# Weight quarters summed by accumulating transfers, with the next product's operands traced behind the preceding product

## The chip, the cores and the metric

One core of a Trainium2 chip runs the whole program in one launch. The metric is the device time of the execution in microseconds; lower is better.

## The reference, cut to what matters

512 tokens of width 1024 pass two networks of two layers each, in fp32. The parts around the change are the two kinds of feed-forward layers:

```python
D_FF = -(-(8 * D_MODEL) // (3 * 256)) * 256      # 2816
D_FF_2 = 4 * D_MODEL

def swiglu_ffn(x, w_gate, w_up, w_down):          # first network, both layers
    return (jax.nn.silu(x @ w_gate) * (x @ w_up)) @ w_down

def sq_relu_mlp(h, w_up, w_down):                 # second network, both layers
    u = jax.nn.relu(h @ w_up)
    return (u * u) @ w_down
```

Around them stand mixers, cross attention, sliding-window attention, norms and the residual adds, which the change does not touch.

## The kernel before, in words

Every fp32 product runs as three matmuls of a rounded high half and the remainder (`mm3`: hi x hi at L180, hi x lo at L181, lo x hi at L182; which side is loaded as weights differs). So every operand is split: the high half is a copy on ScalarE (L152, `Copy` to fp32r), the low half a subtraction on VectorE (L153), both in `split`. Weights with a norm's gain are split by `chunk` at L172 (ScalarE) and L173 (VectorE), two 128x512 instructions each.

Weights are loaded in blocks of 512 KB, 256 rows by 512 columns, by SP (L161 in `chunk`, L202 in `raw2`) into `raw`, a pool of 5 buffers, and split into `w`, a pool of 4 (`wsplit`). A buffer is free when the split, or the product, that read it is done. PSUM has 5 banks `mm` and 3 banks `aux` (`xbank`). POOL has its own queue for transfers.

`down_steps` multiplies 1024 hidden columns by 1024 rows of the down weights with 7 products instead of 8: both matrices are cut in quarters (`a11` to `a22`, `block(i, j)`), and products are made of sums of quarters (`s1`, `s2`, `chain`) and added to the residual by `out` (`resid`, L429 and L431). Each product is 24 matmuls. In the order of the program they are called 1, 2, 5, 6, 7, 3 and 4 here. The operands of products 5, 6, 7 and 4 need sums of weight quarters: VectorE takes them at L294 (W01 - W00 into `chain`), L305 (W11 - `chain`), L315 (W11 - W01) and L331 (W10 - `chain`), each 128x1024 and twice a product, for the two halves of a quarter. 18 weight blocks are loaded a call.

It is a generator. `weave` runs one piece of it, up to the next `yield`, then `per` steps of the side generator `hidden`, which computes the next 1024 columns of the hidden layer: `lin_steps` with 24 matmuls a step and, after the last of four steps, the evacuation of the four banks: `silu` at L922 in `ffn`, `relu` at L1048 and a squaring at L1053 in `mlp`. `ffn` calls it twice a layer with two side steps a piece (L941), `mlp` three times a layer with one (L1065): 4 and 6 calls in all.

The order on each engine comes from a scheduler that walks the program in the order in which it is traced. A block under `high_priority(offset=120)` counts as traced 120 instructions earlier. Within an engine everything runs in that fixed order, so an instruction that waits holds all behind it on its engine.

Of the kernel before, what the change touches and what calls it, by code (L numbers as in the profile page):

```python
# [14 lines left out]
ALU = mybir.AluOpType  # L15
AX = mybir.AxisListType

ALPHA = 4.0 ** 0.25
# [54 lines left out]
class Net:  # L73
# [158 lines left out]
        for _ in side:  # L232
            pass

    def down_steps(self, h, W, k0, first, ahead=120):

        nc = self.nc
        early = lambda: self.tc.high_priority(offset=ahead)
        lo, hi = slice(0, 256), slice(256, 512)
        a11, a21, a12, a22 = h[0][:, :, lo], h[0][:, :, hi], h[1][:, :, lo], h[1][:, :, hi]
        sums = self.slot([128, 2, 4, 256], name="sum")
        s1, s2 = sums[:, 0], sums[:, 1]
        chain = self.slot([128, 4, 512], name="chain")
        tt = nc.vector.tensor_tensor

        def left(src):  # L250
            d = self.slot([128, 2, 4, 256], F32R, "A")
            self.split(d[:, 0], d[:, 1], src)
            return d

        def block(i, j):
            return [self.raw2(W, k0 + 4 * i + k, 512 * j) for k in (0, 2)]

        def halves(t):
            return [t[:, 0:2], t[:, 2:4]]

        def product(d, us, banks, start):
            for t in range(2):
                tk = slice(t * 128, t * 128 + 128)
                for k in range(4):
                    u = us[k // 2]
                    self.mm3(banks[t], d[:, 0, k, tk], d[:, 1, k, tk], u[:, 0, k % 2], u[:, 1, k % 2],
                             start and k == 0, k == 3, skip_group_check=not start)

        def out(i, j, banks):
            for t in range(2):  # L270
                self.resid(2 * i + t, banks[t], 512 * j, first and (i, j) not in done)
            done.add((i, j))

        done = set()
        with early():
            d = left(a11)
            us = [self.wsplit(b) for b in block(0, 0)]
        x = [self.xbank([128, 512]) for _ in range(2)]
        product(d, us, x, True)
        out(0, 0, x)  # L280
        yield
        with early():
            d = left(a12)
            us = [self.wsplit(b) for b in block(1, 0)]
        y = [self.xbank([128, 512]), self.bank([128, 512])]
        product(d, us, y, True)
        out(0, 0, y)
        yield
        with early():
            tt(s1, a21, a22, ALU.add)  # L290
            d = left(s1)
            us = []
            for c, p, q in zip(halves(chain), block(0, 1), block(0, 0)):
                tt(c, p, q, ALU.subtract)  # L294
                us.append(self.wsplit(c))
        z = [self.xbank([128, 512]), self.bank([128, 512])]
        product(d, us, z, True)
        out(1, 1, z)
        yield
        with early():  # L300
            tt(s2, s1, a11, ALU.subtract)
            d = left(s2)
            us = []
            for c, p in zip(halves(chain), block(1, 1)):
                tt(c, p, c, ALU.subtract)  # L305
                us.append(self.wsplit(c))
        product(d, us, x, False)
        out(0, 1, x)
        yield
        with early():  # L310
            tt(a21, a11, a21, ALU.subtract)
            d = left(a21)
            us = []
            for p, q in zip(block(1, 1), block(0, 1)):
                tt(p, p, q, ALU.subtract)  # L315
                us.append(self.wsplit(p))
        product(d, us, x, False)
        out(1, 1, x)
        yield
        with early():  # L320
            tt(a12, a12, s2, ALU.subtract)
            d = left(a12)
            us = [self.wsplit(b) for b in block(1, 1)]
        product(d, us, z, False)
        out(0, 1, z)
        yield
        with early():
            d = left(a22)
            us = []
            for c, p in zip(halves(chain), block(1, 0)):  # L330
                tt(c, p, c, ALU.subtract)  # L331
                us.append(self.wsplit(c))
        product(d, us, x, False)
        out(1, 0, x)
        yield

# [86 lines left out]
        nc.vector.scalar_tensor_tensor(dst, x, mv[:, 0:1], g, ALU.subtract, ALU.mult)  # L423
        nc.vector.scalar_tensor_tensor(dst, dst, rs[:, 0:1], b, ALU.mult, ALU.add)

    def resid(self, t, ps, c0, first=False):
        r = self.r[t][:, c0:c0 + 512]
        if first:
            self.nc.vector.scalar_tensor_tensor(r, r, ALPHA, ps, ALU.mult, ALU.add)  # L429
        else:  # L430
            self.nc.vector.tensor_tensor(r, r, ps, ALU.add)  # L431

# [840 lines left out]
```

## Time and profile before

| | |
|---|---|
| median of 3 runs | 2495.14 us (2490.13 to 2496.63) |
| the profiled execution | 2487.76 us, span 2486.0 us |
| mean granted TensorE clock in it | 0.986 |
| busy: TensorE, VectorE, ScalarE, POOL | 97%, 61%, 41%, 7% |
| moved by DMA | 291.92 MB, mean 117 GB/s |
| the chain that ended last | 89% TensorE, 6% VectorE, 3% ScalarE |

The span is the stretch from the first to the last instruction; the execution's own time has 1.8 us around it. The granted clock is a share of TensorE's full 2.4 GHz; 0.50 is 1.2 GHz. L12 is line 12 of the kernel.

### The profile page before, as it was taken

To read this page: it belongs to the slowest core of one execution; us is meant where nothing else is said; L and a number is where in the kernel's file an instruction comes from. 1 tells how busy PE (TensorE), PEld (TensorE's weight loads), DVE (VectorE), ACT (ScalarE), POOL (GpSimd) and SP (SyncE) were. 2 spreads that over 40 slices of the span, in tenths; PEclk is the share of its full clock that TensorE was granted. 3 is DMA by queue.
4 is the path that set the end of the run, shared out by engine and by line. 5 is a ranking of instruction groups with operands and counts; after the bars stand their busy time and mean duration, and the time that the engine had idled before them with its cause. 6 is when DMAs were issued, how large, how long until landed. Compare 5 with 4: busy or idle time off the path is not lost.

```text
span 2486.0 us, 30362 instructions
## 1 busy us (share of the span) xinstructions
PE 2416.0 (97%) x12094; PEld 2012.8 (81%) x12094; DVE 1514.2 (61%) x1994; ACT 1026.8 (41%) x1620; POOL 180.0 (7%) x219
## 2 busy tenths in 40 slices
PE   8989999999999999999999999999999999999998
PEld 8877787887878997887878786888888877888887
DVE  4898666346466766446467432457876467477784
ACT  3653343223333343223334733444444456444443
POOL 1251300000000000000001002200000100000000
PEclk9999999999999999999999999999999989999999
DMA  6323122234334332235334123325543421254451
GB/s 233 110 97 107 54 94 77 88 113 165 110 129 154 127 130 76 94 102 170 110 125 149 61 85 34 102 86 185 186 161 128 152 68 36 69 170 154 151 186 68
DMA packets 148990, 291.92 MB, mean 117 GB/s; under 512 B 9449, under 2 KB 15909, under 8 KB 148592
## 3 DMA queue, kind: packets, MB, share of 16 engines
q1 hardware_dynamic: 146176, 282.17, 34.2%
q0 software_dynamic: 2096, 6.76, 1.4%
q8 instruction: 95, 1.56, 0.3%
q10 hardware_dynamic: 576, 1.05, 0.1%
q14 instruction: 47, 0.39, 0.0%
HBM read 286.77 MB, written 6.32 MB: 118 GB/s over the span
## 4 chain that ended last, share of the span: by engine, by line
PE 89%; DVE 6%; ACT 3%; issue 1%; DMA 0%; POOL 0%; SPq 0%; POOLq 0%; ACTq 0%; DVEq 0%
PE mm L180 23%; PE mm L181 23%; PE mm L182 23%; PE aux L180 5%; PE aux L182 5%; PE aux L181 5%; DVE acc L662 2%; PE aux L391 2%; DVE w L153 1%; PE aux L718 1%; PE mm L745 1%; ACT w L152 1%; PE mm L742 1%; PE aux L1195 1%; DVE bn L412 0%
## 5 line engine op out<-in xcount | busy, mean ns | idle before, releaser
L180 PE MATMUL mm<-xTh,w 128*128 128x512 f32 (+1 forms) x1696 | 614.6, 365 | 4.6 <-ACT w L152 4.1
L181 PE MATMUL mm<-xTl,w 128*128 128x512 f32 (+1 forms) x1696 | 616.7, 364 | 2.2 <-DVE xTl L153 2.2
L182 PE MATMUL mm<-xTh,w 128*128 128x512 f32 (+1 forms) x1696 | 596.0, 361 | 0.0
L153 DVE TENSOR_TENSOR w<-raw,w 128x1024 fp32r<-128x1024 f32 (+1 forms) x286 | 341.2, 1196 | 352.8 <-ACT w L152 352.4
L152 ACT ACTIVATE w<-raw 128x1024 fp32r<-128x1024 f32 (+1 forms) x286 | 293.4, 1029 | 602.6 <-PE mm L182 429.0
L180 PEld LDWEIGHTS mm<-xTh,w 128*128 128x128 f32 x1696 | 321.4, 190 | 58.0 <-ACT w L152 7.1
L181 PEld LDWEIGHTS mm<-xTl,w 128*128 128x128 f32 x1696 | 322.5, 190 | 51.4 <-DVE xTl L153 2.4
L182 PEld LDWEIGHTS mm<-xTh,w 128*128 128x128 f32 x1696 | 319.2, 189 | 48.8
L173 DVE SCALAR_TENSOR_TENSOR w<-raw,gains_T,w 128x512 fp32r<-128x512 f32 (+1 forms) x200 | 139.1, 738 | 118.1 <-ACT w L172 117.6
L172 ACT ACTIVATE w<-raw,gains_T 128x512 fp32r<-128x512 f32 (+1 forms) x200 | 131.1, 707 | 132.5 <-PE mm L182 118.5
L180 PE MATMUL aux<-w,A 128*128 128x512 f32 x440 | 172.8, 393 | 13.3 <-ACT w L152 13.3
L181 PE MATMUL aux<-w,A 128*128 128x512 f32 x440 | 172.5, 392 | 0.0
L182 PE MATMUL aux<-w,A 128*128 128x512 f32 x440 | 168.9, 391 | 0.0
L181 PE MATMUL mm<-w,xTh 128*128 128x512 f32 (+1 forms) x352 | 135.0, 383 | 0.0
L182 PE MATMUL mm<-w,xTl 128*128 128x512 f32 (+1 forms) x352 | 134.4, 384 | 0.0
L180 PE MATMUL mm<-w,xTh 128*128 128x512 f32 (+1 forms) x352 | 134.1, 384 | 0.0
L152 ACT ACTIVATE w<-chain 128x1024 fp32r<-128x1024 f32 x60 | 63.1, 1059 | 118.7 <-PE mm L182 75.0
L180 PEld LDWEIGHTS aux<-w,A 128*128 128x128 f32 x440 | 83.4, 190 | 32.3 <-ACT w L152 15.0
L181 PEld LDWEIGHTS aux<-w,A 128*128 128x128 f32 x440 | 83.6, 190 | 17.6
L182 PEld LDWEIGHTS aux<-w,A 128*128 128x128 f32 x440 | 83.4, 190 | 17.5
L431 DVE TENSOR_TENSOR r<-r,mm 128x512 f32<-128x512 f32 x76 | 51.6, 684 | 64.6 <-PE mm L182 64.5
L153 DVE TENSOR_TENSOR w<-chain,w 128x1024 fp32r<-128x1024 f32 x60 | 72.8, 1223 | 24.9 <-ACT w L152 24.6
(358 smaller groups left out, 4161.6 us busy)
## 6 DMA issues: line engine op xcount, KB each, us to landing
raw<-in_w_down SPq DMA_DIRECT2D x124, 512.0 KB, 3.3
raw<-in_ffn_wd SPq DMA_DIRECT2D x84, 512.0 KB, 3.4
raw<-in_w_up SPq DMA_DIRECT2D x64, 512.0 KB, 3.7
raw<-in_ffn_wg SPq DMA_DIRECT2D x40, 512.0 KB, 3.6
raw<-in_ffn_wu SPq DMA_DIRECT2D x40, 512.0 KB, 4.0
raw<-in_ab_w_in SPq DMA_DIRECT2D x24, 512.0 KB, 3.9
raw<-in_a_w_in SPq DMA_DIRECT2D x24, 512.0 KB, 3.5
raw<-in_xa_wk SPq DMA_DIRECT2D x16, 512.0 KB, 3.6
```

Source lines behind the costliest of these rows:

```text
L152: self.nc.scalar.activation(hi, src, AF.Copy)
L153: self.nc.vector.tensor_tensor(lo, src, hi.bitcast(F32), ALU.subtract)
L172: nc.scalar.activation(u[:, 0, i], raw[:, i], AF.Identity, scale=g)
L173: nc.vector.scalar_tensor_tensor(u[:, 1, i], raw[:, i], g, u[:, 0, i].bitcast(F32), ALU.mult, ALU.subtract)
L180: nc.tensor.matmul(ps, lh, rh, start=start, stop=False, **kw)
L181: nc.tensor.matmul(ps, lh, rl, start=False, stop=False, **kw)
L182: nc.tensor.matmul(ps, ll, rh, start=False, stop=stop, **kw)
L391: self.nc.tensor.transpose(ps[:, j, :], src[:, j * 128:j * 128 + 128], self.ident)
L431: self.nc.vector.tensor_tensor(r, r, ps, ALU.add)
L662: nc.vector.scalar_tensor_tensor(dst, src, col, dst, ALU.mult, ALU.add)
L718: nc.tensor.matmul(d[:, h - h0, :], ke[rows, t, h * 128:h * 128 + 128], vh(t, h)[rows, :], start=True, stop=True)
L742: nc.tensor.matmul(o, P[:, h, :], vh(t, h), start=True, stop=False)
```

## The change

Weight sums leave VectorE. `add` lets a transfer of POOL's queue load a quarter and add it to what lies in the buffer (`accum_op=ALU.add`). Since such a transfer only adds, the signs turn: `s1` is a21 - a22, `a12` becomes a12 + s2, and the products with the sums of products 6 and 7 are subtracted from the residual (`out(..., ALU.subtract)`). `chain` starts with a plain load of W01 by SP, to which W00 is added for product 5, W11 for product 6 and W10 for product 4; product 7's sum is W01 added into the `raw` block of W11. Of 18 weight blocks a call, 10 are loaded by SP and 8 by POOL. Each product's operands are now made by a function (`p1` to `p4`) that is called right behind the preceding product and its `out`, ahead of the `yield`, with `high_priority` by 60 instead of 120.

```diff
-    def down_steps(self, h, W, k0, first, ahead=120):
+    def down_steps(self, h, W, k0, first, ahead=60):
...
+        def plain(i, j):
+            return [self.wsplit(b) for b in block(i, j)]
...
-        def out(i, j, banks):
+        def out(i, j, banks, op=ALU.add):
             for t in range(2):
-                self.resid(2 * i + t, banks[t], 512 * j, first and (i, j) not in done)
+                self.resid(2 * i + t, banks[t], 512 * j, first and (i, j) not in done, op)
             done.add((i, j))
...
+        def early(f):
+            with self.tc.high_priority(offset=ahead):
+                return f()
...
+        def add(dst, i, j):
+            for n, c in enumerate(dst):
+                k = k0 + 4 * i + 2 * n
+                nc.gpsimd.dma_start(c, W[k * 128:(k + 2) * 128, 512 * j:512 * j + 512].rearrange(
+                    "(k p) c -> p k c", p=128), accum_op=ALU.add)
+            return [self.wsplit(c) for c in dst]
+
+        def p1():
+            return left(a11), plain(0, 0)
+
+        def p2():
+            return left(a12), plain(1, 0)
+
+        def p5():
+            tt(s1, a21, a22, ALU.subtract)
+            d = left(s1)
+            for n, c in enumerate(halves(chain)):
+                k = k0 + 2 * n
+                nc.sync.dma_start(c, W[k * 128:(k + 2) * 128, 512:1024].rearrange("(k p) c -> p k c", p=128))
+            return d, add(halves(chain), 0, 0)
+
+        def p6():
+            tt(s2, s1, a11, ALU.subtract)
+            return left(s2), add(halves(chain), 1, 1)
+
+        def p7():
+            tt(a21, a11, a21, ALU.subtract)
+            return left(a21), add(block(1, 1), 0, 1)
+
+        def p3():
+            tt(a12, a12, s2, ALU.add)
+            return left(a12), plain(1, 1)
+
+        def p4():
+            return left(a22), add(halves(chain), 1, 0)
+
+        ops = early(p1)
+        product(ops, x, True)
         out(0, 0, x)
+        ops = early(p2)
         yield
-        with early():
-            d = left(a12)
-            us = [self.wsplit(b) for b in block(1, 0)]
         y = [self.xbank([128, 512]), self.bank([128, 512])]
-        product(d, us, y, True)
+        product(ops, y, True)
         out(0, 0, y)
+        ops = early(p5)
         yield
-        with early():
-            tt(s1, a21, a22, ALU.add)
-            d = left(s1)
-            us = []
-            for c, p, q in zip(halves(chain), block(0, 1), block(0, 0)):
-                tt(c, p, q, ALU.subtract)
-                us.append(self.wsplit(c))
         z = [self.xbank([128, 512]), self.bank([128, 512])]
-        product(d, us, z, True)
+        product(ops, z, True)
         out(1, 1, z)
+        ops = early(p6)
         yield
...
-        product(d, us, x, False)
-        out(0, 1, x)
+        product(ops, x, False)
+        out(0, 1, x, ALU.subtract)
...
```

The lines move by 17 behind `down_steps`: `silu` L922 is L939, `relu` L1048 is L1065, the residual adds L429 and L431 are L446 and L448. The accumulating transfers have L290, the plain loads of `chain` L305.

How the order on the engines moves is shown at three places. ScalarE at product 5 of the first feed-forward call, before (`sg<-mm` are the `silu` evacuations of the side step, `A<-sum` the left operand of products 5 and 6, `w<-chain` the weights of product 5):

```order
L152 ACTIVATE w_4448<-raw_4446 128x1024
L922 ACTIVATE sg_4313<-mm_4319 128x512
L922 ACTIVATE sg_4313<-mm_4320 128x512
L922 ACTIVATE sg_4313<-mm_4321 128x512
L152 ACTIVATE A_4480<-sum_4270 128x1024
L922 ACTIVATE sg_4313<-mm_4322 128x512
L152 ACTIVATE A_4590<-sum_4270 128x1024
L152 ACTIVATE w_4492<-chain_4271 128x1024
L152 ACTIVATE w_4496<-chain_4271 128x1024
L152 ACTIVATE w_4529<-raw_4527 128x1024
```

And now:

```order
L152 ACTIVATE A_4313<-sg_4021 128x1024
L152 ACTIVATE A_4418<-sum_4270 128x1024
L152 ACTIVATE w_4329<-raw_4327 128x1024
L152 ACTIVATE w_4362<-raw_4360 128x1024
L152 ACTIVATE w_4425<-chain_4271 128x1024
L152 ACTIVATE w_4428<-chain_4271 128x1024
L152 ACTIVATE w_4433<-raw_4431 128x1024
L152 ACTIVATE w_4462<-raw_4460 128x1024
L152 ACTIVATE w_4527<-chain_4271 128x1024
L939 ACTIVATE sg_4326<-mm_4332 128x512
L152 ACTIVATE A_4522<-sum_4270 128x1024
L152 ACTIVATE A_4622<-sg_3668 128x1024
```

The left operand and both weight halves of product 5 (`w_4425`, `w_4428`), and the first of product 6 (`w_4527`), stand ahead of the first `silu`; before, they stood behind three of the four.

TensorE at product 1 of the first MLP call, before (`mm` with `w_12358` is the next up step, `aux` product 1):

```order
L182 MATMUL mm_12365<-xTh_11622,w_12358 128x512
L180 MATMUL mm_12365<-xTh_11622,w_12358 128x512
L181 MATMUL mm_12365<-xTl_11624,w_12358 128x512
L182 MATMUL mm_12365<-xTh_11622,w_12358 128x512
L180 MATMUL aux_12327<-w_12321,A_12314 128x512
L181 MATMUL aux_12327<-w_12321,A_12314 128x512
L180 MATMUL aux_12328<-w_12321,A_12314 128x512
L181 MATMUL aux_12328<-w_12321,A_12314 128x512
```

And now:

```order
L181 MATMUL mm_12109<-xTl_11553,w_12199 128x512
L182 MATMUL mm_12109<-xTh_11551,w_12199 128x512
L180 MATMUL mm_12110<-xTh_11551,w_12199 128x512
L181 MATMUL mm_12110<-xTl_11553,w_12199 128x512
L182 MATMUL mm_12110<-xTh_11551,w_12199 128x512
L180 MATMUL aux_12242<-w_12251,A_12244 128x512
L181 MATMUL aux_12242<-w_12251,A_12244 128x512
L180 MATMUL aux_12243<-w_12251,A_12244 128x512
L181 MATMUL aux_12243<-w_12251,A_12244 128x512
```

18 matmuls of the next up step stood between the last step of the hidden columns (`w_12271` before, `w_12199` now) and product 1; now product 1 follows that step directly.

ScalarE in the same call, now (`w<-chain` twice is product 5, the next twice product 6, `w<-raw,gains_T` the up weights of the side steps):

```order
L152 ACTIVATE A_12244<-h_11846 128x1024
L1065 ACTIVATE tmp_12234<-mm_12109 128x512
L152 ACTIVATE w_12293<-raw_12288 128x1024
L1065 ACTIVATE tmp_12237<-mm_12110 128x512
L152 ACTIVATE A_12283<-h_12099 128x1024
L172 ACTIVATE w_12299<-raw_12297,gains_T 128x512 x2
L152 ACTIVATE A_12361<-sum_12240 128x1024
L152 ACTIVATE A_12434<-sum_12240 128x1024
L152 ACTIVATE A_12503<-h_11846 128x1024
L152 ACTIVATE w_12368<-chain_12241 128x1024
L152 ACTIVATE w_12371<-chain_12241 128x1024
L172 ACTIVATE w_12376<-raw_12374,gains_T 128x512 x2
```

and POOL's queue there, which had no transfer in this stage before (`raw` is product 7's sum, `chain` x6 the six additions for products 5, 6 and 4):

```order
L422 TENSOR_SCALAR rs_11828<-ss_1523_11825 128x1
L423 TENSOR_TENSOR rs_11828<-rs_11828,half 128x1
L290 DMA raw_12506<-in_w_down 128x2x512
L290 DMA raw_12508<-in_w_down 128x2x512
L290 DMA chain_12241<-in_w_down 128x2x512 x6
L290 DMA raw_13071<-in_w_down 128x2x512
L290 DMA raw_13073<-in_w_down 128x2x512
```

Product 5's splits stand ahead of the up weights of the following step (`w_12376`), and on POOL the two additions for product 7 stand ahead of those for product 5.

## Rows read from the trace of the kernel before

**Rows 1.** The page's first part, the whole span: busy us of each engine (share of the span) and number of instructions; below it the granted TensorE clock in 40 slices of the span, in tenths.

```profile
PE 2416.0 (97%) x12094; PEld 2012.8 (81%) x12094; DVE 1514.2 (61%) x1994; ACT 1026.8 (41%) x1620; POOL 180.0 (7%) x219
...
PEclk9999999999999999999999999999999989999999
```

**Rows 2.** What TensorE waited for, the whole span: operation that waited <- what ended the wait: us in total, times, longest us.

```profile
PE aux L180 <- ACT w L152: 13.3, 4, 3.3
...
PE mm L180 <- ACT w L152: 4.1, 5, 1.1
```

**Rows 3.** Busy time by stretch (us from:to): length, busy us (instructions) of each engine, granted clock, DMA busy share, GB/s.

```profile
560.00:700.00 140.00, 131.58 (x565) 107.31 (x564) 76.58 (x75) 49.54 (x55) 0.00 (x0) 0.97 0.41 135
...
1680.00:1880.00 200.00, 199.89 (x882) 165.14 (x881) 157.24 (x179) 91.82 (x115) 0.00 (x0) 1.00 0.52 176
1960.00:2130.00 170.00, 159.68 (x789) 126.78 (x788) 107.16 (x228) 96.97 (x264) 5.39 (x8) 0.93 0.26 87
2200.00:2400.00 200.00, 200.00 (x884) 165.62 (x883) 157.11 (x179) 89.80 (x113) 0.00 (x0) 1.00 0.53 179
```

**Rows 4.** The timeline around the first stall: start, duration, engine, line, operation, out<-in, and in brackets the idle time before it and what ended that.

```profile
560.14 1.96 ACT L922 ACTIVATE sg<-mm 128x512 f32<-128x512 f32 x3 [13.22 <-PE mm L182]
...
561.75 0.39 PE L182 MATMUL mm<-xTh,w 128*128 128x512 f32 x1
562.00 1.05 ACT L152 ACTIVATE A<-sum 128x1024 fp32r<-128x1024 f32 x1
562.94 0.59 ACT L922 ACTIVATE sg<-mm 128x512 f32<-128x512 f32 x1
...
563.42 1.06 ACT L152 ACTIVATE A<-sum 128x1024 fp32r<-128x1024 f32 x1
564.37 2.00 ACT L152 ACTIVATE w<-chain 128x1024 fp32r<-128x1024 f32 x2
...
565.47 0.80 PE L180 MATMUL aux<-w,A 128*128 128x512 f32 x1 [3.33 <-ACT w L152]
...
567.36 0.79 PE L180 MATMUL mm<-xTh,w 128*128 128x512 f32 x1 [0.67 <-ACT w L152]
...
572.17 0.39 PE L181 MATMUL aux<-w,A 128*128 128x512 f32 x1
```

**Rows 5.** The same stretch by the microsecond, and the six microseconds behind the second and the fourth stall; columns as in rows 3.

```profile
561.00:562.00 1.00, 1.00 (x6) 0.60 (x4) 0.00 (x0) 0.92 (x3) 0.00 (x0) 1.00 0.97 369
...
565.00:566.00 1.00, 0.53 (x1) 0.50 (x2) 1.00 (x2) 1.00 (x2) 0.00 (x0) 0.63 0.00 0
...
571.00:572.00 1.00, 1.00 (x4) 0.81 (x3) 1.00 (x2) 0.00 (x0) 0.00 (x0) 0.50 0.99 381
572.00:573.00 1.00, 1.00 (x5) 0.82 (x5) 1.00 (x2) 0.00 (x0) 0.00 (x0) 0.95 0.51 176
...
699.00:705.00 6.00, 5.25 (x12) 4.13 (x13) 5.93 (x6) 1.64 (x2) 0.00 (x0) 0.50 0.35 112
...
1262.00:1268.00 6.00, 5.14 (x12) 3.80 (x12) 6.00 (x6) 2.12 (x3) 0.00 (x0) 0.50 0.28 83
```

**Rows 6.** The timeline at the start of the MLP's first `down_steps` call, of ScalarE, TensorE and VectorE in turn; columns as in rows 4.

```profile
1656.43 1.34 ACT L172 ACTIVATE w<-raw,gains_T 128x512 fp32r<-128x512 f32 x2 [3.70 <-PE mm L182]
...
1661.00 1.05 ACT L152 ACTIVATE A<-h 128x1024 fp32r<-128x1024 f32 x1
...
1661.67 0.39 PE L180 MATMUL mm<-xTh,w 128*128 128x512 f32 x1
...
1665.75 0.39 PE L180 MATMUL aux<-w,A 128*128 128x512 f32 x1
...
1662.09 1.23 DVE L153 TENSOR_TENSOR A<-h,A 128x1024 fp32r<-128x1024 f32 x1 [0.26 <-ACT A L152]
...
1663.83 1.22 DVE L153 TENSOR_TENSOR w<-raw,w 128x1024 fp32r<-128x1024 f32 x1
```

**Rows 7.** DMA transfers: out<-in, queue, count, KB each, median us from issue to landing, in the stretches 1680 to 1720, 1980 to 2010 and 2040 to 2060; and an issue on POOL in the timeline.

```profile
raw<-in_w_down SPq DMA_DIRECT2D x10, 512.0 KB, 4.1
...
bias<-rep POOLq DMA_DIRECT2D x2, 512.0 KB, 7.2
...
bias<-rep POOLq DMA_DIRECT2D x2, 512.0 KB, 4.5
...
1983.68 1.52 POOL L1144 DMA_DIRECT2D bias<-rep  x2 [17.40 <-DMA rep<-rv]
```

**Rows 8.** VectorE by line, the whole span: line, operation, out<-in, count | busy us, mean ns of one | idle before, what ended it.

```profile
L331 DVE TENSOR_TENSOR chain<-raw,chain 128x1024 f32<-128x1024 f32 x20 | 24.5, 1224 | 14.8 <-DMA raw<-in_w_down 7.9 <-DMA raw<-in_ffn_wd 6.9
L315 DVE TENSOR_TENSOR raw<-raw,raw 128x1024 f32<-128x1024 f32 x20 | 24.4, 1222 | 5.9 <-DMA raw<-in_ffn_wd 5.6 <-DMA raw<-in_w_down 0.2
L305 DVE TENSOR_TENSOR chain<-raw,chain 128x1024 f32<-128x1024 f32 x20 | 24.1, 1223 | 0.0
L294 DVE TENSOR_TENSOR chain<-raw,raw 128x1024 f32<-128x1024 f32 x20 | 24.1, 1221 | 0.0
```

**Rows 9.** What TensorE waited for in 2000 to 2120 us, the second block's attention (columns as in rows 2), and two stretches of it (columns as in rows 3).

```profile
PE aux L1195 <- DVE s L1181: 1.7, 1, 1.7
...
2024.00:2026.00 2.00, 0.20 (x2) 0.00 (x0) 1.79 (x3) 1.15 (x3) 0.00 (x0) 1.00 0.00 0
2026.00:2034.00 8.00, 7.82 (x25) 5.71 (x26) 6.00 (x10) 2.67 (x9) 0.00 (x0) 0.51 0.20 68
```

More of the change, by code (lines that the diff above doesn't have):

```diff
@@ L233, in weave @@
             pass
-    def down_steps(self, h, W, k0, first, ahead=120):
+    def down_steps(self, h, W, k0, first, ahead=60):
         nc = self.nc
-        early = lambda: self.tc.high_priority(offset=ahead)
         lo, hi = slice(0, 256), slice(256, 512)
@@ L248, in down_steps @@
         tt = nc.vector.tensor_tensor
+        done = set()
         def left(src):
@@ L256, in block, with product @@
             return [self.raw2(W, k0 + 4 * i + k, 512 * j) for k in (0, 2)]
+        def plain(i, j):
+            return [self.wsplit(b) for b in block(i, j)]
         def halves(t):
             return [t[:, 0:2], t[:, 2:4]]
-        def product(d, us, banks, start):
+        def product(ops, banks, start):
+            d, us = ops
             for t in range(2):
@@ L267, in product @@
                              start and k == 0, k == 3, skip_group_check=not start)
-        def out(i, j, banks):
+        def out(i, j, banks, op=ALU.add):
             for t in range(2):
-                self.resid(2 * i + t, banks[t], 512 * j, first and (i, j) not in done)
+                self.resid(2 * i + t, banks[t], 512 * j, first and (i, j) not in done, op)
             done.add((i, j))
-        done = set()
-        with early():
-            d = left(a11)
-            us = [self.wsplit(b) for b in block(0, 0)]
+        def early(f):
+            with self.tc.high_priority(offset=ahead):
+                return f()
@@ L278, in down_steps @@
         x = [self.xbank([128, 512]) for _ in range(2)]
-        product(d, us, x, True)
+        def add(dst, i, j):
[8 more added lines that the diff above has]
+            return left(a12), plain(1, 0)
@@ L287, in down_steps @@
         out(0, 0, y)
+        ops = early(p5)
         yield
-        with early():
-            tt(s1, a21, a22, ALU.add)
-            d = left(s1)
-            us = []
-            for c, p, q in zip(halves(chain), block(0, 1), block(0, 0)):
-                tt(c, p, q, ALU.subtract)
-                us.append(self.wsplit(c))
         z = [self.xbank([128, 512]), self.bank([128, 512])]
-        product(d, us, z, True)
+        product(ops, z, True)
         out(1, 1, z)
+        ops = early(p6)
@@ L299, in down_steps @@
         yield
[L300 to L306, printed above, removed]
-        product(d, us, x, False)
-        out(0, 1, x)
-        yield
[L310 to L316, printed above, removed]
@@ L317, in down_steps @@
-        product(d, us, x, False)
-        out(1, 1, x)
-        yield
[L320 to L324, printed above, removed]
+        product(ops, x, False)
+        out(0, 1, x, ALU.subtract)
+        ops = early(p7)
+        yield
+        product(ops, x, False)
+        out(1, 1, x, ALU.subtract)
+        ops = early(p3)
+        yield
+        product(ops, z, False)
@@ L325, in down_steps @@
         out(0, 1, z)
+        ops = early(p4)
         yield
[L327 to L333, printed above, removed]
+        product(ops, x, False)
         out(1, 0, x)
@@ L424, in ln_tile, with resid @@
         nc.vector.scalar_tensor_tensor(dst, dst, rs[:, 0:1], b, ALU.mult, ALU.add)
-    def resid(self, t, ps, c0, first=False):
+    def resid(self, t, ps, c0, first=False, op=ALU.add):
         r = self.r[t][:, c0:c0 + 512]
         if first:
-            self.nc.vector.scalar_tensor_tensor(r, r, ALPHA, ps, ALU.mult, ALU.add)
+            self.nc.vector.scalar_tensor_tensor(r, r, ALPHA, ps, ALU.mult, op)
         else:
-            self.nc.vector.tensor_tensor(r, r, ps, ALU.add)
+            self.nc.vector.tensor_tensor(r, r, ps, op)
     def hgrn_mixer(self):
```

## The prediction

> **What bounds the kernel now.** I read the busy shares first. TensorE works 97% of the span, VectorE 61%, ScalarE 41% [rows 1]. So 70 us of TensorE's idle time are all that can be taken back without removing matmuls, beside what the lower clock costs, and the change removes no matmul: 7 products of 24 stay 7 products of 24. The next view is what TensorE's idle time ended on. The largest entry is the change's own place: the first matmul of a product waits for ScalarE's splitting copy `w` at L152, 13.3 us in 4 times, and right behind it four of the five waits of 4.1 us in all [rows 2]. Where these lie is told by the stages. In the stretch 560 to 700 us, the two `down_steps` calls of the first block's feed-forward layer, TensorE is busy 131.6 of 140 us. In 1680 to 1880 and 2200 to 2400, where the MLP's calls run, it is busy 199.9 and 200.0 of 200 us [rows 3]: there is nothing to win there, only something to lose.
>
> One of the four stalls, seen closely [rows 4]: at 560.14 ScalarE begins the `silu` evacuations (L922), which wait for the side step's last matmuls. Behind the first three stand the split of the left operand `A<-sum`, a fourth `silu`, another `A<-sum`, and only then the split of product 5's weights `w<-chain` at 564.37. TensorE's last matmul before the gap starts at 561.75, the next at 565.47: 3.33 us idle, and two matmuls later 0.67 more. The granted clock, 1.00 until then, goes to 0.50 from 565 on, the 1.2 GHz level, and is back at 572 [rows 5]; the stretches behind the other stalls show 0.50 as well (first and last of three shown, [rows 5]).
>
> **What one such stall costs.** Matmuls follow each other every 0.227 us at full clock: 18 of them lie between 1661.67 and 1665.75 [rows 6]. The first after the gap was due at 561.75 + 0.23 = 561.98, the fourteenth at 561.98 + 13 x 0.227 = 564.93. It started at 572.17 [rows 4]. Loss 7.2 us, of which 4.0 are idle and the rest half clock. Four places: 29 us.
>
> **The change, part by part.**
>
> *Order of the operands, FFN.* Each product's operands are now traced behind the preceding product, before the side step. In the order of the changed program `A<-sum` and both `w<-chain` of product 5 stand ahead of the four `silu` that delayed them. They then wait only for the slot of an earlier matmul and for data. The weight quarter now comes by a plain load on SP and an accumulating one on POOL, in front of which TensorE has some 60 matmuls left, 14 us; a 512 KB load takes 3 to 4 us on SP and 4.5 to 7.2 on POOL [rows 7]. That fits, so I take all four stalls as gone: **-29 us**. Bounds: 0 (all come back elsewhere) and -29.
>
> *VectorE's 80 subtractions.* L294, L305, L315, L331: 24.1 + 24.1 + 24.4 + 24.5 = 97 us leave VectorE [rows 8]. No wait of TensorE names these lines as its end and VectorE has idle time in every stage [rows 3], so I cost them at 0. What stood behind them (splits, the residual adds) only gets earlier.
>
> *Signs.* `s1` and `a12` turn their sign, two products are subtracted in `resid`: the same instructions with another operation, 0.
>
> *Product 1 of the six MLP calls.* Before, 18 matmuls of the next up step stood between the last step and product 1 (1661.67 to 1665.75). In the changed order product 1 comes at the place of 1661.67, and its left operand `A<-h` still stands behind two evacuations: it starts at 1661.00 and lasts 1.05 us, so it is done at 1662.05, 0.4 us too late [rows 6]. TensorE must still load it as weights, and its low half on VectorE ends at 1662.09 + 1.23 = 1663.32, a little after the fourth matmul wants it. I take 0.7 us each, 6 x 0.7 = **+4 us**; bounds 0 and 1.5 each.
>
> *Product 5 of the six MLP calls, the uncertain term.* In front of the accumulation stands a chain. SP issues the second quarter of product 7 and the two plain `chain` loads only once VectorE has split the block whose buffer they follow, which in the trace ends at 1663.83 + 1.22 = 1665.05 [rows 6]. At 4.1 us per load in this stage [rows 7], three behind each other, the second `chain` half lands at about 1671.5. POOL, busy with about 0.76 us per issue (1.52 for two, [rows 7]), has the two accumulations into product 7's blocks ahead of it in its queue. On the other side ScalarE has `w<-chain` twice ahead of the split of the next up step's weights. With product 1 at 1662.4, that step follows 72 matmuls later, at 1678.7; take off 0.7 us for the up weights' first half (1.34 for two) and 1.05 for the split, and the second accumulation must have landed by 1676.9. That leaves some 5.5 us from issue to landing. No accumulating DMA is in this trace. The nearest row is `bias<-rep`, the same 512 KB by POOL's queue: 4.5 us where the other queues rested, 7.2 beside SP's loads [rows 7]. The MLP has SP's loads beside it, so I take 7.2: 1.7 us late, 6 x 1.7 = **+10 us**. Lower bound 4.5 us, no wait at all. Upper bound twice 7.2, 14.4 us: 8.9 late, and with the clock 12 a call, +72. Product 6 has one more accumulation, started by product 5's split, with a few microseconds to spare; it becomes late only where product 5 is late already.
>
> The Trainium skill ("Collectives: The Full Stack", Part 3, the bandwidth ceiling) says that a reducing transfer is slower than a copy because it reads two sources for each write, about half the copy's rate, and not because of the addition. By it each accumulation would take a second reading of 512 KB, an estimate of 1.5 us more, and the term would be 6 x 3.2 = 19 instead of 10. No run here shows it yet.
>
> *Elsewhere.* The order outside these calls is the same but for the second block's attention near 2000 to 2110 us, where TensorE waits 1.7 us for VectorE's `s` at one of several tight places now [rows 9] and the new order has fewer of them: **-3 us**, between -6 and +6.
>
> **Sum:** -29 + 4 + 10 - 3 = -18. The profiled execution took 2487.8 us (span 2486.0), the sum 2469.8. The median of the runs shown lies 7.4 above that execution, at 2495.1; so 2477.
>
> **The rivals.**
>
> *The accumulations are slow (slower).* Place: the two `w<-chain` at product 5 of the six MLP calls, with the up weights and all that follows on ScalarE behind them. An idle stretch there costs the clock as well, about 3 us each, as in the FFN. With a landing time of 10 us it is 4.5 late + 3.1 = 7.6 a call, 46 in all: -29 + 4 + 46 - 3 = +18, **2513**. It decides from 28 / 6 = 4.7 us lost per call. For it: nothing in before shows such a transfer, and the MLP's DMA share is already 0.52 against 0.41 in the FFN [rows 3]. Against it: half of the engines' time is free.
>
> *The accumulations are as late as forecast, but the clock falls too (no change).* Between 2024 and 2026 TensorE stood 1.8 us, and the granted clock behind it was 0.51 [rows 9]. Then each call loses 1.7 + 3.1 = 4.8, 29 in all: +1, **2496**.
>
> *Everything lands in time.* POOL's transfers at 4.5 to 5.5 us: -29 + 4 + 0 - 3 to -9, **2462** to 2467.
>
> *The FFN's wait only moves.* In the new order the split of product 6's first half (`w<-chain` after the next accumulation) stands ahead of the first `silu`; if that accumulation is late, ScalarE holds the evacuations and TensorE waits for banks at the same price: 0 + 4 + 10 - 3 = +11, **2506**. Against it: from product 5's split to that `silu` TensorE has some 75 matmuls, 17 us.
>
> *VectorE holds up POOL's issuing.* The rows show POOL issuing in 0.76 us, in a stage where VectorE is busy 107 of 170 us [rows 3, 7]; in the MLP it is busy 157 of 200. If each of the two issues had to wait for one VectorE operation of 1.2 us, 2.4 more per call, 14 in all: -4, **2491**, or 2509 with the clock. The Trainium skill ("SBUF — State Buffer", "SBUF: two separate sides") describes such a trap: while VectorE runs in a mode that takes both port pairs, GpSimd cannot write the descriptors of its transfers. By that rule the 1.2 us operations would have to be of that mode; no row here shows a POOL transfer held up by one.
>
> **How the numbers follow.** Forecast 0.47 (its own range 2468 to 2487), all in time 0.09: faster 0.56. Clock falls 0.17 and a part of VectorE's hold 0.02: same 0.19. Slow accumulations 0.20, FFN wait moved 0.03, the rest of the hold 0.02: slower 0.25. About 0.3%, 7.5 us, is what a measurement of this kernel tells from no change. The range 2461 to 2513 takes in the forecast, the quick case, the clock and the slow case up to a landing time of 10 us.
>
> **What would show it.** Right: the wait of `aux` at L180 on `w` at L152 is gone from 560 to 700 and 1120 to 1270, with a granted clock of 1.00 there; VectorE's busy time is down by 97 us; POOL's `chain` and `raw` transfers land in 7 to 8 us; the MLP stretches show short waits for `w` behind those transfers and for `A`, with the clock still 1.00. Wrong: a clock below 1.00 in the MLP stretches, landing times of 10 us or more, or the FFN's idle time unchanged under another name.

## The result

The changed kernel takes 2517.95 us (median of 4 runs, 2513.8 to 2524.4), the kernel before 2493.99 (4 runs). The ratio is 1.010, 95% interval 1.0073 to 1.0126: slower by 24 us. The profiled execution took 2513.8 us, its span is 2512.0, that of before 2486.0: 26 us between two single executions, which the profile below explains. One run of all those on record, of the kernel with product 5's sum on VectorE, took 3422.03 us at a mean granted clock of 0.651, and the median of that kernel is given without it.

The page's first part, to be laid beside [rows 1]: VectorE's busy time is down by 94 us, with 80 instructions fewer, and TensorE's share falls from 97 to 96%.

```profile
PE 2419.4 (96%) x12094; PEld 2009.8 (80%) x12094; DVE 1420.6 (57%) x1914; ACT 1024.1 (41%) x1620; POOL 277.2 (11%) x299
```

What TensorE waited for over the whole span; columns as in [rows 2]. The wait of `aux` on `w` at L152, 13.3 us before, is no longer in the list. A wait for the up weights, split at L172, leads it now, and the new wait at product 1 for `A` has 2.1 us in all:

```profile
PE mm L180 <- ACT w L172: 39.7, 8, 7.3
...
PE aux L180 <- ACT A L152: 2.1, 8, 0.3
```

By stretch, columns as in [rows 3]:

```profile
560.00:700.00 140.00, 140.00 (x619) 115.94 (x618) 71.91 (x73) 49.85 (x55) 12.10 (x10) 1.00 0.55 143
1120.00:1270.00 150.00, 150.00 (x664) 124.20 (x663) 69.78 (x71) 45.41 (x48) 10.28 (x9) 1.00 0.52 139
1680.00:1880.00 200.00, 186.81 (x798) 151.78 (x797) 122.01 (x145) 84.47 (x107) 19.34 (x16) 0.97 0.57 148
1960.00:2130.00 170.00, 163.62 (x832) 129.15 (x831) 109.28 (x232) 101.10 (x274) 6.12 (x10) 0.97 0.26 87
2200.00:2400.00 200.00, 179.08 (x756) 145.44 (x755) 112.96 (x133) 77.03 (x96) 21.74 (x18) 0.95 0.61 152
```

The two feed-forward stretches are full, 140.00 of 140 and 150.00 of 150 us, with the clock at 1.00. The MLP stretches, which were full before, have lost 13.1 and 20.9 us of TensorE's busy time, and their clock is 0.97 and 0.95. So the change did what it should in one place and lost more in another.

**The place of the loss.** The MLP's first call. TensorE's two rows that end an idle time, and two beside the first (start, duration, line, operation, in brackets the idle time and what ended it): product 1 begins 0.44 us behind the place that the pace of 0.227 us gives it (1635.69 + 0.23 = 1635.92), of which the profile counts 0.28 as idle, and the up step behind product 2 waits 6.23 us, from 1653.34 on.

```profile
1635.69 0.39 PE L182 MATMUL mm<-xTh,w 128*128 128x512 f32 x1
1636.36 0.50 PE L180 MATMUL aux<-w,A 128*128 128x512 f32 x1 [0.28 <-ACT A L152]
...
1637.62 0.49 PE L182 MATMUL aux<-w,A 128*128 128x512 f32 x1
...
1659.57 0.79 PE L180 MATMUL mm<-xTh,w 128*128 128x512 f32 x1 [6.23 <-ACT w L172]
```

What it waits for, on ScalarE: nothing runs from 1646.26 to 1655.23, then the two splits of product 5's sum, each ended by a transfer, and only then the up weights.

```profile
1645.20 1.06 ACT L152 ACTIVATE A<-h 128x1024 fp32r<-128x1024 f32 x1
1655.23 1.06 ACT L152 ACTIVATE w<-chain 128x1024 fp32r<-128x1024 f32 x1 [8.97 <-DMA chain<-in_w_down]
1657.85 1.06 ACT L152 ACTIVATE w<-chain 128x1024 fp32r<-128x1024 f32 x1 [1.56 <-DMA chain<-in_w_down]
1658.81 1.32 ACT L172 ACTIVATE w<-raw,gains_T 128x512 fp32r<-128x512 f32 x2
```

The transfers that ScalarE waits for are issued by POOL, two for product 7's sum first, then the two for product 5:

```profile
1636.89 1.26 POOL L290 DMA_DIRECT2D raw<-in_w_down  x1 [44.53 <-DMA raw<-in_w_down]
1644.92 1.21 POOL L290 DMA_DIRECT2D raw<-in_w_down  x1 [6.77 <-DVE sum L309]
1646.15 1.21 POOL L290 DMA_DIRECT2D chain<-in_w_down  x1
1647.57 1.19 POOL L290 DMA_DIRECT2D chain<-in_w_down  x1 [0.21 <-issue]
```

The issues on SP, where the two plain loads of `chain` stand behind product 7's blocks:

```profile
1633.03 6.67 SPq L202 DMA_DIRECT2D raw<-in_w_down  x2
1639.75 1.15 SPq L305 DMA_DIRECT2D chain<-in_w_down  x2
1647.11 0.37 SPq L161 DMA_DIRECT2D raw<-in_w_up  x1
```

The first addition to the chain takes from 1646.15 to 1655.2, 9.1 us, the second from 1647.57 to 1657.85, 10.3 us. To be in time, the second split had to begin at 1653.34 - 1.06 - 0.7 = 1651.6; it began 6.3 us later, which is the idle time of 6.23. The page's table of transfers has a median for all 36 additions to the chain in the MLP, those for products 6 and 4 too:

```profile
chain<-in_w_down POOLq DMA_DIRECT2D x36, 512.0 KB, 7.9
```

While the three transfers of 1644.92 to 1647.57 are under way, the DMA engines are full (columns as in [rows 3], the second last is their busy share):

```profile
1646.50:1657.00 10.50, 6.84 (x31) 5.33 (x29) 7.00 (x8) 1.06 (x1) 2.05 (x2) 0.96 1.04 199
1657.00:1660.00 3.00, 0.43 (x1) 0.43 (x2) 1.60 (x2) 2.15 (x3) 1.19 (x1) 0.50 0.12 18
```

They hold three additions, product 7's second and product 5's two, and the up weights' own plain load of 1647.11.

From within the idle time on, the granted clock is at its lower level, 1.2 GHz, for some 7 us, as it was behind the FFN stalls:

```profile
1652.00:1654.00 2.00, 1.34 (x6) 0.76 (x5) 0.82 (x2) 0.00 (x0) 0.00 (x0) 1.00 1.09 237
1654.00:1659.00 5.00, 0.00 (x0) 0.00 (x0) 1.28 (x2) 2.20 (x3) 1.16 (x1) 0.72 0.67 129
1659.00:1663.00 4.00, 3.43 (x8) 2.75 (x9) 2.49 (x3) 1.13 (x2) 1.24 (x2) 0.50 0.90 147
1663.00:1665.00 2.00, 2.00 (x10) 1.61 (x10) 0.00 (x0) 1.06 (x1) 0.00 (x0) 1.00 1.01 190
```

The other five calls show the same, with 5.5 to 7.4 us of idle time, 37.9 in all six. With each goes a stretch at 0.50 of 6.8 us, of which 3.0 to 5.6 us lie beside running matmuls.

The account by stage comes from the starts of the matmuls, 12094 in each trace: the change only reorders them within a stage, so the time of the matmul of the same number at a stage's borders tells what the stage gained or lost. The columns are matmul number, its start before and after, the difference, and how much of it arose since the line above, with the name of that stage:

```
 2750   510.5   512.6   +2.1   start, programs alike
 3750   752.0   739.3  -12.7   -14.8  first FFN
 5750  1104.8  1092.1  -12.8    0.0
 6500  1289.4  1262.1  -27.3   -14.5  second FFN
 8250  1646.7  1621.0  -25.7   +1.6
 9500  1930.5  1932.9   +2.5  +28.2  first MLP layer
10500  2139.4  2134.2   -5.2   -7.6  attention
12000  2457.2  2483.2  +26.0  +31.2  second MLP layer
```

-29 in the FFN, +59 in the MLP, -8 in the attention and +4 where the programs are alike make the 26 us.

### The profile page after: what moved, and what is told of

Same layout as the page of the kernel before. It is cut to its first block, busy times and chain, and to the rows that moved or that the text cites. A ratio compares the mean times of both kernels' runs of the same rounds, so it can differ in the third digit from the quotient of the medians.

```text
span 2512.0 us, 30330 instructions
## 1 busy us (share of the span) xinstructions
PE 2419.4 (96%) x12094; PEld 2009.8 (80%) x12094; DVE 1420.6 (57%) x1914; ACT 1024.1 (41%) x1620; POOL 277.2 (11%) x299
## 3 DMA queue, kind: packets, MB, share of 16 engines
q1 hardware_dynamic: 124416, 240.22, 29.2%
q0 software_dynamic: 23856, 48.71, 11.2%
q8 instruction: 95, 1.56, 0.3%
## 4 chain that ended last, share of the span: by engine, by line
PE 84%; DVE 7%; DMA 4%; ACT 3%; issue 2%; POOL 1%; SPq 0%; POOLq 0%; ACTq 0%; DVEq 0%
PE mm L180 22%; PE mm L181 22%; PE mm L182 22%; PE aux L180 4%; PE aux L182 4%; PE aux L181 4%; DMA chain<-in_w_down 3%; PE aux L408 2%; DVE acc L679 2%; DVE w L153 1%; PE aux L735 1%; PE mm L762 1%; PE mm L759 1%; ACT w L172 1%; DVE bn L429 0%
## 5 line engine op out<-in xcount | busy, mean ns | idle before, releaser
L180 PE MATMUL mm<-xTh,w 128*128 128x512 f32 (+1 forms) x1696 | 617.1, 366 | 40.7 <-ACT w L172 39.7
L182 PE MATMUL mm<-xTh,w 128*128 128x512 f32 (+1 forms) x1696 | 579.8, 362 | 0.0
L152 ACT ACTIVATE w<-raw 128x1024 fp32r<-128x1024 f32 (+1 forms) x286 | 292.9, 1030 | 613.1 <-PE mm L182 520.8
L172 ACT ACTIVATE w<-raw,gains_T 128x512 fp32r<-128x512 f32 (+1 forms) x200 | 130.8, 707 | 128.9 <-PE mm L182 117.6
L152 ACT ACTIVATE w<-chain 128x1024 fp32r<-128x1024 f32 x60 | 63.7, 1062 | 168.6 <-DMA chain<-in_w_down 97.7
L448 DVE TENSOR_TENSOR r<-r,aux 128x512 f32<-128x512 f32 x96 | 65.4, 681 | 90.0 <-PE aux L182 89.9
```

Source lines behind the costliest of these rows:

```text
L152: self.nc.scalar.activation(hi, src, AF.Copy)
L172: nc.scalar.activation(u[:, 0, i], raw[:, i], AF.Identity, scale=g)
L180: nc.tensor.matmul(ps, lh, rh, start=start, stop=False, **kw)
L182: nc.tensor.matmul(ps, ll, rh, start=False, stop=stop, **kw)
L448: self.nc.vector.tensor_tensor(r, r, ps, op)
```

## The experiments

Theory A: an addition makes the transfer read its destination too, so it holds the DMA engines about twice as long, and several run one behind another. Theory B: product 5's transfers are only issued too late. Theory C: POOL's queue is slow, whatever its transfers do. The first four kernels part these, and the two halves of the change from each other. The time of the kernel before in the same series stands behind each.

**Additions left out.**

```diff
-                    "(k p) c -> p k c", p=128), accum_op=ALU.add)
+                    "(k p) c -> p k c", p=128))
```

> The eight transfers of POOL's queue stay where they are in every queue, but load without adding, so the sums of the weight quarters are left out. Theory A (an addition makes the transfer read its destination too and hold the DMA engines about twice as long, and several such transfers run one behind another): product 5's transfers in the MLP land in 4.5 to 6 us instead of 9 to 10, TensorE's six waits of 6.3 us shrink to 0 to 3 us, time 2460 to 2485. Theory B (the transfers are only issued too late, behind SP's late plain loads): landing may fall, but most of the wait stays, 4 to 5 us each, time 2495 to 2510. Theory C (POOL's queue itself is slow, whatever the transfer does): landing 9 to 10 us as before, time 2510 to 2520.

Measured: 2489.93 us (before 2491.9; ratio 0.9993, 0.998 to 1.0006). So 28 of the 47 us that lie between the changed kernel (2518) and the next one below, with its sums on VectorE (2471), come with the addition alone. The page's queues, packets, MB and share of 16 engines' span, of the changed kernel:

```profile
q1 hardware_dynamic: 124416, 240.22, 29.2%
q0 software_dynamic: 23856, 48.71, 11.2%
```

and of this one:

```profile
q1 hardware_dynamic: 124416, 240.22, 30.0%
q0 software_dynamic: 13616, 48.71, 6.3%
```

The same 48.71 MB take 11.2% of 2512.0 us, 281 us, with the additions and 6.3% of 2489.8, 157 us, without: 124 us over 80 transfers, 1.56 us each. A plain 512 KB load of SP holds the engines for 29.2% of 2512.0 us x 0.524 / 240.22 = 1.60 us. An added one therefore costs twice a plain one, as theory A has it: the 80 alone, without the 1.4% of 2486.0 us that POOL's other transfers take in the kernel before, 35 us, have 3.1 us each. Smaller packets are not the reason. The trace has an added transfer in packets of 2 KB, of 178 ns in the median, where the same transfer without the addition has 4 KB and 159 ns; but SP's plain loads go in 2 KB packets too, and theirs take 84 ns. The Trainium skill ("Collectives: The Full Stack", Part 3, the bandwidth ceiling) names the reason, two reads for a write; the number here agrees with it, while the reading itself is not in the profile.

Theory C falls: the landing time is 4.8 us in place of 7.9. But theory B is not out. The wait is still there, at most 3.3 us:

```profile
PE mm L180 <- ACT w L172: 17.0, 8, 3.3
```

POOL's issues and ScalarE's splits in the first MLP call. Product 1 begins at 1643.4 here, so the two transfers are issued 9.3 and 10.6 us behind it (9.8 and 11.2 in the changed kernel), and land 7.0 and 7.8 us later (9.1 and 10.3):

```profile
1652.70 0.72 POOL L290 DMA_DIRECT2D chain<-in_w_down  x1 [0.51 <-issue]
1653.93 0.72 POOL L290 DMA_DIRECT2D chain<-in_w_down  x1 [0.51 <-DMA chain<-in_w_down]
```

```profile
1659.70 1.06 ACT L152 ACTIVATE w<-chain 128x1024 fp32r<-128x1024 f32 x1 [6.43 <-DMA chain<-in_w_down]
1661.71 1.06 ACT L152 ACTIVATE w<-chain 128x1024 fp32r<-128x1024 f32 x1 [0.96 <-DMA chain<-in_w_down]
```

By stage, as above, the two MLP layers lose 15.1 and 14.7 us here, against 28.2 and 31.2: half of the loss is the addition's, and half is there with plain transfers as well. The forecast by theory A alone, 2460 to 2485, was too low by 5 us.

**Sums on VectorE again, in the new place.** All quarters are loaded by SP; VectorE adds.

```diff
-                nc.gpsimd.dma_start(c, W[...], accum_op=ALU.add)
+                tt(c, c, self.raw2(W, k0 + 4 * i + 2 * n, 512 * j), ALU.add)
...
-                nc.sync.dma_start(c, W[...])
-            return d, add(halves(chain), 0, 0)
+            for c, p, q in zip(halves(chain), block(0, 1), block(0, 0)):
+                tt(c, p, q, ALU.add)
```

> The new place of the operands and the turned signs alone: all weight quarters are loaded by SP and summed by VectorE again. If the loss of the changed kernel is the accumulating transfers' alone (theories A and C), the six MLP waits are gone, the four FFN waits stay gone, and the time is 2450 to 2465. If the new place itself harms the MLP (rival: operands earlier in ScalarE's order hold the up weights behind them, whoever makes the sums), waits of 2 us or more for the up weights stay in the MLP and the time is 2480 to 2510.

Measured: 2471.14 us (before 2491.9; ratio 0.9928, 0.9901 to 0.9955). The new place of the operands alone is worth 21 us, and all but 8 us of the MLP's loss were the transfers'. The time is 6 us above the forecast's upper end. By stage the FFN gives 28 us back, the attention 3, and the two MLP layers still lose 4 each: that is what the place itself costs there, some 5.5 us at product 1 of the six calls and the rest in waits of at most 0.9 us in the third call of each layer. The waits in 1620 to 1900 and the stretches (columns as above):

```profile
PE aux L180 <- ACT A L152: 1.0, 4, 0.3
PE mm L180 <- ACT w L172: 0.9, 1, 0.9
```

```profile
560.00:700.00 140.00, 140.00 (x619) 116.02 (x618) 79.07 (x79) 49.75 (x55) 0.00 (x0) 1.00 0.46 145
...
1680.00:1880.00 200.00, 198.21 (x869) 162.29 (x868) 150.44 (x175) 89.21 (x114) 0.00 (x0) 1.00 0.48 160
2200.00:2400.00 200.00, 198.21 (x868) 162.35 (x867) 151.71 (x175) 89.08 (x114) 0.00 (x0) 1.00 0.51 169
```

**Accumulating transfers in the old place.** Each `early(...)` stands right before its product, `ahead` is 120.

```diff
-        ops = early(p5)
         yield
+        ops = early(p5)
```

(and so for the other five)

> The accumulating transfers alone: each product's operands are traced right before their product again, with the priority of 120. If the new place is what took away the four FFN waits, they are back or replaced by a wait for the accumulated quarter, 4 times 3 us or more with a clock of 0.50 behind them. In the MLP the transfers still take 8 to 10 us; the first four of POOL's queue there are no longer product 7's two, so theory A expects waits of 2 to 6 us in six calls, time 2500 to 2530. If the transfers were as good as plain loads, 2490 to 2500.

Measured: 2511.81 us (before 2491.9; ratio 1.0088, 1.0065 to 1.0112). The FFN waits are back, the first now 5.2 us, with two in 560 to 705:

```profile
PE aux L180 <- ACT w L152: 8.5, 2, 5.2
```

```profile
560.00:700.00 140.00, 134.17 (x582) 110.18 (x581) 64.42 (x65) 43.43 (x48) 10.86 (x9) 0.98 0.55 137
1120.00:1270.00 150.00, 140.84 (x604) 114.94 (x602) 71.49 (x71) 48.05 (x53) 13.39 (x11) 0.97 0.54 137
...
1680.00:1880.00 200.00, 196.94 (x860) 160.38 (x859) 128.15 (x151) 84.24 (x105) 26.67 (x22) 1.00 0.68 169
```

In the first MLP layer the forecast was too high: the waits are 0.6 us or less and the stretch has 196.9 of 200 us busy. Product 5's two additions stand ahead of product 7's second one on POOL in this order. By stage the FFN gains nothing against before (+0.8 and +1.1), the MLP layers lose 5.2 and 7.9, the attention 2; 4.7 of the profiled execution's 24 us lie in its first 510 us, where the programs are alike. So the two halves work on each other: with the sums by transfer the new place loses 59 us in the MLP, the old one 13, and with the sums on VectorE the new one 8.

**Two additions fewer.** Product 7's sum is loaded twice and added on VectorE.

```diff
-            return left(a21), add(block(1, 1), 0, 1)
+            for p, q in zip(block(1, 1), block(0, 1)):
+                tt(p, p, q, ALU.add)
```

> As the changed kernel, but product 7's sum is loaded twice by SP and added by VectorE, so two of the eight accumulating transfers a call are gone, those that stand ahead of product 5's on POOL's queue. Theory A (transfers of twice the time behind one another): product 5's second half lands about 3 us earlier, the MLP waits fall from 6.3 to about 3 us, time 2480 to 2500. Theory B (late issue alone): the plain loads of the chain stay behind product 7's second block on SP, so waits stay at 5 to 6 us, time 2505 to 2520. Theory C: the same as B.

Measured: 2507.33 us (before 2491.9; ratio 1.0069, 1.005 to 1.0087), inside theory B's range for the time. The wait itself fell as theory A has it, from 6.3 to 3.9 us in the mean of the six, about the one transfer that stood ahead:

```profile
PE mm L180 <- ACT w L172: 25.3, 8, 4.2
```

The clock still falls behind all six, and the MLP loses 45 us by stage in place of 59, so the time moved by less than theory A's sum.

**Product 5's transfers ahead.** The plain loads and the first additions are issued in `p1`, and no longer in `p5`.

```diff
         def p1():
-            return left(a11), plain(0, 0)
+            ops = left(a11), plain(0, 0)
+            for n, c in enumerate(halves(chain)):
+                k = k0 + 2 * n
+                nc.sync.dma_start(c, W[...])
+            add(halves(chain), 0, 0)
+            return ops
```

> As the changed kernel, with the plain load and the first addition of product 5's sum issued with product 1's operands, ahead of its splits, so that on SP and POOL they stand ahead of product 7's second block. The transfers take as long as before. If the MLP's loss is transfers in series against too short a room (theories A and B together), the room grows by about 3.5 us and one addition is out of the queue: the six waits fall from 6.3 to 0 to 2 us, time 2465 to 2485. If the additions themselves are the limit in the sum of the stage (the DMA engines cannot carry them at all), the waits stay at 4 us or more there or come back at products 6 and 7, time 2500 to 2515.

Measured: 2474.48 us (before 2488.75; ratio 0.9945, 0.9926 to 0.9964). POOL's issues, ScalarE's splits in the first MLP call, and the wait left over the span:

```profile
1634.42 1.27 POOL L290 DMA_DIRECT2D raw<-in_w_down  x1 [44.83 <-DMA raw<-in_w_down]
1636.17 2.53 POOL L290 DMA_DIRECT2D chain<-in_w_down  x2 [0.47 <-issue]
1643.67 1.19 POOL L290 DMA_DIRECT2D raw<-in_w_down  x1 [4.97 <-DVE r L453]
```

```profile
1645.54 1.06 ACT L152 ACTIVATE w<-chain 128x1024 fp32r<-128x1024 f32 x1 [4.92 <-DMA chain<-in_w_down]
1648.40 1.05 ACT L152 ACTIVATE w<-chain 128x1024 fp32r<-128x1024 f32 x1
```

```profile
PE aux L180 <- ACT w L152: 6.2, 6, 2.2
```

The additions are issued at 1636.17, before product 7's second block, and take as long as ever: the first lands at 1645.5, 9.4 us later. Now that is in time. What is left is a wait of at most 2.2 us at product 6, whose addition can only start when product 5's split has read the chain.

**The fourth corner**: product 5's transfers ahead, and no additions.

> Product 5's transfers issued with product 1's operands, and POOL's transfers load without adding, so the sums are left out: the fourth corner beside the changed kernel, its form without additions, and its form with product 5's transfers ahead. Theory: the wait is the transfers' time beyond the room, so with more room the additions cost only what is left over: no wait over 1 us at product 5 or 6, time 2462 to 2474, 0 to 10 us under the form with additions. Rival: POOL's queue costs of its own, whatever room there is: 2480 or more.

Measured: 2466.26 us (before 2493.35; ratio 0.9901, 0.9873 to 0.9929). No wait at product 5 or 6 is left; the longest for split weights in the MLP is one for the up weights:

```profile
PE mm L180 <- ACT w L172: 1.8, 2, 0.9
```

The four corners are 2518 and 2490 (with and without additions, issued late) and 2474 and 2466 (issued early). They come from four series, in which the kernel before lies between 2488.75 and 2493.99, so a difference of a few us between them is not safe. By stage, in the profiled executions, the MLP loses 59.4, 29.8, 17.7 and 8.0 us against before: the additions cost 30 us where there is no room and 10 where there is, and the early issue brings 42 and 22. The 8.0 left are the place's own, as in the kernel with the sums on VectorE. Theories A and B are both needed, and they are not independent: only the part of the transfer beyond the room is paid.

**Additions in the FFN alone.** `add` takes VectorE's way in the MLP's calls.

> Accumulating transfers in the four FFN calls only; in the six MLP calls SP loads all quarters and VectorE adds them. Theory: in the FFN the room was enough (waits gone with either form of the sum), so this equals the kernel with all sums on VectorE, 2463 to 2478, and no wait over 1 us in either stage. If taking the sums off VectorE were worth something in the FFN, it would be faster than 2463 by 3 us or more.

Measured: 2470.76 us (before 2488.75; ratio 0.9928, 0.9902 to 0.9953), the same as with all sums on VectorE. The stretches:

```profile
560.00:700.00 140.00, 140.00 (x620) 115.95 (x619) 69.10 (x70) 49.55 (x55) 13.29 (x11) 1.00 0.56 144
1120.00:1270.00 150.00, 150.00 (x663) 124.24 (x663) 73.44 (x75) 48.52 (x53) 10.93 (x9) 1.00 0.52 139
1620.00:1900.00 280.00, 277.87 (x1217) 227.62 (x1216) 205.77 (x236) 123.47 (x156) 1.24 (x3) 1.00 0.49 160
```

VectorE is busy 69.1 of 140 us in the first stretch, against 79.1 with the sums on it, and TensorE 140.00 in both: taking these 32 of the 80 sums off VectorE is worth nothing.

**Product 5's transfers ahead and product 7's sum on VectorE.** Both edits from above.

> Product 5's transfers issued with product 1's operands and product 7's sum on VectorE, so only the six additions to the chain are left. Theories A and B: no wait over 1 us for the up weights in the MLP, time 2455 to 2475. If late plain loads on SP are what remains (20 loads by SP or more a call), waits of 1 to 3 us remain, time 2475 to 2490.

Measured: 2471.06 us (before 2488.75; ratio 0.9927, 0.9899 to 0.9955), as theories A and B had it: no wait in the MLP is over 0.9 us.

**Product 5's sum on VectorE, the others added by transfers.**

```diff
-            return d, add(halves(chain), 0, 0)
+            for c, p, q in zip(halves(chain), block(0, 1), block(0, 0)):
+                tt(c, p, q, ALU.add)
```

> Product 5's sum taken by VectorE from two plain loads side by side, the sums of products 6, 7 and 4 by accumulating transfers. If product 5 alone has too little room, the six MLP waits are gone, 2450 to 2470. If the later products are close to their limit as well (product 6's addition starts when product 5's split is done), waits of 1 to 4 us stand there instead, 2475 to 2500. In the second block's attention the order is nearer to the changed kernel's than to the other's, which theory puts at some 10 us less than in the kernel with all sums on VectorE.

Measured: 2489.43 us (before 2488.75; ratio 1.0004, 0.9985 to 1.0023). The second of the forecast's cases: the waits stand at the following product, 13.9 us in all:

```profile
PE aux L180 <- ACT w L152: 13.9, 7, 3.6
```

VectorE's sum comes early enough for product 5, but product 6's addition still starts behind product 5's split and lands after a median of 8.7 us in the MLP. The chain is a series of transfers, and each link has the room of one product.

Three forms beat both kernels and are the same within their intervals: all sums on VectorE (2471.1), additions in the FFN alone (2470.8), and additions with product 5's ahead and product 7's on VectorE (2471.1). Product 5's transfers ahead, with all additions (2474.5), is not told from them by its interval. The simplest is the first.

## Why the prediction was wrong

The forecast was 2477, faster; measured 2518, slower, and above the range of 2461 to 2513.

- *FFN stalls, -29*: right. Both stretches are full, the clock is 1.00, and the kernels with VectorE's sums in the new place show that it is the place that did it. The room was ample: that [rows 7] has 4.1 us for a load on SP, and not 3 to 4 as written there, changes nothing.
- *97 us off VectorE at 0*: right as far as the runs show it. 32 of the 80 sums taken off it in the FFN (35 us less of VectorE's busy time in the whole span) and 60 of them in the kernel of both edits (67 us less) leave 2470.8 and 2471.1 us, against 2471.1 with all 80 on it.
- *Product 1, +4*: right in place and mechanism, and a little small. It begins 0.44 us late for `A`, its fifth matmul another 0.35 us late for A's low half (1637.62, where four steps of 0.227 us from 1636.36 lead to 1637.27), and over its 24 matmuls the starts are 0.93 us behind, 5.5 in the six calls. The kernel with VectorE's sums in the new place loses 8 in the MLP; the rest, some 2.5, are waits of 0.2 and 0.9 us in the third call of each layer and what follows on them, which the prediction had not seen.
- *Attention, -3*: the waits there went from 10.1 to 6.0 us, as forecast; the stage gained 7.6 in the two profiled executions, with the clock, more than the bound of 6. With VectorE's sums in the new place 9.5 us of the waits stay and the gain is 3.
- *Product 5 in the MLP, +10*: this step failed. The place, the queue and the instruction that would wait were as told, but the term measures 59 - 8 = 51: 38 us idle and 13 at the lower clock. Three things were mis-sized. First, the landing time: 7.2 us, from a pair of plain loads. The kernel without additions has 7.0 and 7.8 in this very place, so for a plain pair the row was right; with additions it is 9.1 and 10.3. I priced one transfer, while POOL's queue holds product 7's second addition and product 5's first ahead of the last, each of 3.1 us on the engines, and the up weights' load of 1.6 us runs beside them: 10.9 us of work, and the engines were full for 10.5. The rows of the order ahead of the prediction show that queue, and I named it without paying for it. By the rule of the Trainium skill that the prediction cites ("Collectives: The Full Stack", Part 3, the bandwidth ceiling) I had an estimate of 1.5 us to add for one transfer. The runs give 1.56 for one; the landing rose by 2.1 and 2.5 us, since the transfers ahead have it as well. Second, the issue: the second addition was issued 11.2 us behind product 1 and not 9.1. SP's two plain loads of the chain landed in a median of 6.3 us in this place and not in 4.1, and my 1671.5 left their overlap unworked: three landings of 4.1 us in a row from 1665.05 would have been 1677.4. For the first call, 1.7 of the forecast + 3.1 + 2.1, less the 0.7 by which the up weights were due later than I had worked out, are 6.2, the idle time measured. Third, the clock: I took a wait of 1.7 us, which may pass without a drop, and so had nothing of the 13 in the sum.
- *The rivals*: the slow accumulations, 2513 with a landing time of 10 us and a chance of 0.20, were what happened; the price per call, 7.6, was still below the 8.6 measured (51.4 us over six calls). The FFN's wait did not move. That VectorE holds up POOL was not seen: POOL's issue takes 1.2 us with the addition and 0.72 without, beside the same work of VectorE.

## What to carry to other kernels

A sum moved into a transfer is off an engine that nobody waited for and onto a path in series: load, then add, then split. Price it by the engines' time of every transfer ahead of it in the queue and beside it, and not by its own landing time, and compare with the room from its issue to the first instruction behind its reader. Before moving work, try the reordering alone: here it was the whole gain.

## What the runs showed that was not expected

An accumulating transfer is longer to issue: 1.2 us of POOL against 0.72 for the same transfer without the addition, and the software queue has 23856 packets against 13616, 128 more for each of the 80.

A wait has no fixed price in clock. In the kernel without additions the idle times at the six places are 3.1, 1.7, 2.3, 3.3, 2.0 and 2.9 us; the granted clock fell to 0.50 behind the first, third and fourth, not behind the others. And in the first 510 us, where all these programs are alike, the profiled executions lie between 0.6 us ahead of before's and 9.1 us behind it, so a single execution of this kernel can't be read to better than that as a whole; the differences by stage can.
